# A diffusion backbone layer on one core: raw weights in a ring of six blocks, a later place for the post norm's transposes, reordered chains at both ends

## The chip, the core and the metric

The kernel runs on one core of a Trainium2 chip. A core has five engines with a queue of instructions each: TensorE (PE, matrix products; its weight loads are shown apart as PEld), VectorE (DVE), ScalarE (ACT), GpSimd (POOL) and SyncE (SP, which here only issues DMAs). An engine takes its instructions strictly in order and waits on semaphores for the others. The time is the device time of one execution in microseconds; the number that counts is the median of several runs.

## The reference

One layer for 512 latent tokens (8 rows of 64) and 256 context tokens, width 1024, all in float32:

```python
sh, sc, gt = _modulation(c, w_mod[i], b_mod[i])
h = _rmsnorm(x, pre_g[i]) * (1.0 + sc[:, None, :]) + sh[:, None, :]
parts = _split_in(h @ w_in[i])                 # 10 parts of 1024 columns
q, k, v = rope(parts[4]), rope(parts[5]), parts[6]     # 16 heads of 64
attn = _neighbourhood_attention(q, k, v, k_c, v_c, rpb[i])
y_a = (silu(z_a) * b_gate * _dwconv3(c_gate * x_in, conv_w, conv_b)) @ w_out_conv
y_b = (silu(z_b) * attn) @ w_out_attn
merged = sigmoid(g_a) * y_a + sigmoid(g_b) * y_b
x = x + gt[:, None, :] * _rmsnorm(merged @ w_o, post_g[i])
```

The attention of a token reaches over a window of 8 x 16 tokens and all context keys in one softmax. The context tokens go through the same modulation and give keys and values only.

## The kernel before

**Precision.** Each float32 operand of a product is split into a high part H (rounded to the matmul's fp32r type by an ACT copy) and a low part L (DVE, source minus H); a product is three matmuls, H·H, H·L and L·H. `split` (lines 65 to 76) does it; a line 68 or 71 in the profile is therefore a split of anything.

**Weights.** The input and output projections come in chunks of two units of 128 columns, for all 1024 rows: 1 MB each. `Chunk` (line 84) loads a chunk as two halves `raw` of 512 KB (rows 0 to 511 and 512 to 1023; line 90), in a pool of three such buffers. A half holds, for each of its four row blocks, 256 columns; its first and last 128 columns are the blocks b11, b12 (first half) and b21, b22 (second half). There are two kinds of chunk:

- *unpaired*: `split` (line 92) makes H and L of each half at once, 128 x 1024.
- *paired* (`first`, `second`, `pair`): the two units are computed together by a scheme of seven block products instead of eight. `first` splits b11, adds b12, splits the sum, splits b21, adds b22 and splits that sum; `second` splits what is left: T3 (from b12), T4 (from b21) and B22 (from b22), and B12 ahead of them where `keep` is set. The sums are made in place in the raw blocks.

A half's buffer can be written again when the last instruction that reads or changes either of its blocks is done. `Chunks` (line 129) goes through the list `order`: it loads the next chunk in the middle of the present one (`more`) and calls its `first` one attention block later (`behind`). The split weights `w` lie in four buffers.

**Stages.** (1) In `with tc.manual_schedule` (line 456), PE, DVE, ACT and SP keep the order of the program: x is loaded and normalised, transposed on PE, scaled and shifted with the modulation (`m`, line 542), split into `hx`, and multiplied in the same loop with the first six units of weights (`steps`, line 444; weights `fraw`, split into `fH` and `fL`). The modulation itself is a dot product of w_mod's rows with silu(c) on DVE (`condition`, line 397). `crow` is c, `sp` a table of small per-channel constants; both are loaded on SP's queue (lines 457 and 459). (2) Four convolution channels, the context's modulation. (3) 64 attention blocks (8 pairs of heads, 2 heads, 4 column blocks), with the projections of the next pair filled in between by `plan`. (4) The merge: for each of 8 column blocks j (line 938) the two output projections are gated and added; beside it the weights of w_o are loaded (`load_block`), and gate and post norm's gain are combined into one vector `gains` (line 974). At j == 6 that vector is spread over all partitions: eight copies on DVE (line 989), eight PE transposes (990), two ACT copies into `gpost` (991). (5) The output projection by the same scheme of seven products (`tokens`, `both`, lines 1004 to 1017), with squares, sums and the residual (`squares`, `partial`, `close`).

Outside stage 1 a planner orders each engine's queue: it goes through a model of the run with a cost for each instruction, and gives an engine the first instruction in program order that is ready at that point of the model. On the chip the order then stands, whatever is late.

Of the kernel before, what the change touches and what calls it, by code (L numbers as in the profile page):

```python
# [15 lines left out]
P = 128  # L16
# [11 lines left out]
def layer(ctx: ExitStack, tc, xp, ctxt, ctxT, cc, wmod, small, wfirst, win, wout, wo, rel, tab, out):  # L28
# [9 lines left out]
    class Banks:  # L38


        def __init__(self, *tags):
            self.tags, self.n = tags, 0
# [38 lines left out]
    def wtile(shape):  # L81
        return wp.tile(shape, F32R, name="w", bufs=4)

    class Chunk:


        def __init__(self, src):
            self.raws = [wp.tile([P, 4, 256], F32, name="raw", bufs=3) for _ in range(2)]
            for i, raw in enumerate(self.raws):
                nc.sync.dma_start(raw, src[:, 4 * i:4 * i + 4])  # L90

        def split(self):
            t = [wtile([P, 4, 2, 256]) for _ in range(2)]
            for x, raw in zip(t, self.raws):
                split(x[:, :, 0], x[:, :, 1], raw)
            k = range(KT)
            return tuple([t[i // 4][:, i % 4, y] for i in k] for y in range(2)) + ([t[i // 4][:, i % 4] for i in k],)

        def first(self, keep=False):
            (b11, b12), (b21, b22) = self.b = [(r[:, :, :P], r[:, :, P:]) for r in self.raws]  # L100
            t, sums = (wtile([P, 2, 2, 4, P]) for _ in range(2))
            split(t[:, 0, 0], t[:, 0, 1], b11)
            nc.vector.tensor_add(b11, b11, b12)
            split(sums[:, 0, 0], sums[:, 0, 1], b11)
            split(t[:, 1, 0], t[:, 1, 1], b21)
            nc.vector.tensor_add(b11, b11, b22)
            split(sums[:, 1, 0], sums[:, 1, 1], b11)
            self.keep = keep
            if not keep:
                nc.vector.tensor_add(b12, b12, b22)  # L110
            nc.vector.tensor_add(b21, b21, b11)
            self.B = {"B11": t[:, 0], "B21": t[:, 1], "T1": sums[:, 0], "T2": sums[:, 1]}
            return self
# [15 lines left out]
    class Chunks:  # L129
# [4 lines left out]

        def load(self, n):
            if n < len(self.srcs) and n not in self.ahead and n not in self.raw:
                self.raw[n] = Chunk(self.srcs[n][0])
                if behind is None:
                    self.ready(n)
                else:  # L140
                    behind.append(lambda: self.ready(n))
# [235 lines left out]
    with ExitStack() as p0:  # L377
# [66 lines left out]
        def steps(k):  # L444
            H, L = first.pop(k)
            for i in range(6):
                cs = slice(i * P, (i + 1) * P)
                nc.tensor.matmul(acc[i], lhsT=H[:, cs], rhs=hx[0][k], start=k == 0, stop=False)  # L448
                nc.tensor.matmul(acc[i], lhsT=L[:, cs], rhs=hx[0][k], start=False, stop=False)  # L449
            for i in range(6):  # L450
                cs = slice(i * P, (i + 1) * P)
                nc.tensor.matmul(acc[i], lhsT=H[:, cs], rhs=hx[1][k], start=False, stop=k == KT - 1)  # L452
# [1 line left out]

        E = mybir.EngineType
        with tc.manual_schedule(engines={E.PE, E.DVE, E.Activation, E.SP}):
            nc.sync.dma_start(crow, cc[0:1].rearrange("o (a n) -> o a n", a=2))
            xn = [load_x(xp, i, f"x{i}", f"u{i}", hp) for i in range(4)]
            nc.sync.dma_start(sp, small)
            for k in range(3):  # L460
                load_slab(k)
                load_first(k)
# [68 lines left out]
            for k in range(KT):  # L531
                cast_first(k)
                condition(k, 0, [1])
                col = cols.pop((k, 0))
                nc.vector.tensor_mul(col[:, 0:1], col[:, 0:1], sp[:, PG + k:PG + k + 1])
                rest_first(k)
                if k == KT - 1:
                    nc.vector.tensor_scalar(out=hcv, in0=sp[:, CW:CW + 32], scalar1=0.5, scalar2=None, op0=ALU.mult)
                if k + 1 < KT:
                    condition(k + 1, 0, [0])  # L540
                m = st.tile([P, S], F32, name="m", bufs=2)
                nc.scalar.activation(m, turned_x.pop(k), AF.Identity, bias=col[:, 1:2], scale=col[:, 0:1])
                split(hx[0][k], hx[1][k], m)
                if k + 3 < KT:
                    load_slab(k + 3)
                    load_first(k + 3)
                elif k == 5:
                    after = Chunk(order[3][0])
                steps(k)
                if k + 2 < KT:  # L550
                    turned_x[k + 2] = turn_x(k + 2)
# [378 lines left out]
    def sums1(q):  # L930

        nc.vector.tensor_sub(raws[q][:, :, h1], raws[2 + q][:, :, h1], raws[q][:, :, h1])
        nc.vector.scalar_tensor_tensor(
            out=raws[q][:, :, h0], in0=raws[q][:, :, h1], scalar=-1.0, in1=raws[q][:, :, h0],
            op0=ALU.mult, op1=ALU.subtract,
        )

    for j in range(KT):
# [28 lines left out]
        if j in (4, 5):  # L967
# [3 lines left out]
            for k in range(4 * j - 16, 4 * j - 12):  # L971
# [3 lines left out]
                    out=t, in0=t, in1=cond, scale=1.0, scalar=sp[:, BM + 16 + k:BM + 17 + k],  # L975
                    op0=ALU.mult, op1=ALU.add, accum_out=gains[:, k:k + 1],
                )
        if j == 6:

            nc.vector.tensor_mul(gains, gains, sp[:, QG:QG + KT])  # L980
            nc.vector.tensor_scalar(out=gains[:, 0:4], in0=gains[:, 0:4], scalar1=0.5, scalar2=None, op0=ALU.mult)
            nc.vector.tensor_scalar(out=gains[:, 4:8], in0=gains[:, 4:8], scalar1=-0.5, scalar2=None, op0=ALU.mult)
            gpost = bp.tile([P, D], F32, name="gpost")
            for i in range(2):
                gb = cv.tile([P, S], F32, name="ta")
                ps = pj()
                for k in range(4):
                    n = 4 * i + k
                    nc.vector.tensor_copy(gb[:, k * P:(k + 1) * P], gains[:, n:n + 1].broadcast_to([P, P]))
                    nc.tensor.transpose(ps[:, k * P:(k + 1) * P], gb[:, k * P:(k + 1) * P], ident)  # L990
                nc.scalar.copy(gpost[:, i * S:(i + 1) * S], ps)
        if j == 5:
            sums1(0)
        if j == 6:
            nc.scalar.activation(const.tile([P, 1], F32, name="dummy2"), G[7][:, 1, :1], AF.Sqrt, bias=eps, scale=0.0)
            wB11 = moving(B11)
# [29 lines left out]
    def snap(dst, ps):  # L1026
        return lambda t: nc.scalar.copy(dst[:, t], ps[t])

    def squares(t, cols, n, src):
        nc.scalar.activation(sq[:, :cols.stop - cols.start], src, AF.Square, accum_out=sums[:, t, n:n + 1])  # L1030
        nc.vector.tensor_mul(ys[t][:, cols], src, gpost[:, cols])

    def added(a, b):
        y = cv.tile([P, S], F32, name="ta")[:, :a.shape[-1]]
        nc.vector.tensor_add(y, a, b)
        return y
# [71 lines left out]
    for i in range(2):  # L1108
        cols = slice(256 * i, 256 * (i + 1))
        if i == 0:  # L1110
            ff = pj()[:, :256]
            tokens(None, a22, wT4, True, 1, cols, ff)
            squares(3, cols, 1, added(U3s[:, 1, cols], ff))
            partial(3, 1, False)
        else:
            tokens(fa[1], a22, wT4, False, 1, cols)
            squares(3, cols, 2, fa[1][:, cols])
# [87 lines left out]
```

## Time and profile before

| what | value |
|---|---|
| median of 3 runs | 710.05 us (708.62 to 710.88) |
| profiled execution | 710.26 us, its span 708.4 us |
| granted TensorE clock | 0.997 |
| PE busy | 693.9 us, 98% |
| DVE busy | 602.1 us, 85% |
| ACT busy | 446.2 us, 63% |
| POOL busy | 66.9 us, 9% |
| loads of raw weights | 90 of 512 KB (74 from w_in, 16 from the output projections) |

A row of the timeline is: start in us, duration in us, engine, line, operation, output and inputs, number of instructions merged, and in brackets the idle time of the engine before it with what ended it. SPq is SP's queue, which is where a DMA is issued. In the view of waits, a row has the waiting instruction, what it waited for, the total in us, how often, and the longest. In groups by line, the figures after the bar are busy time in us, the mean of one in ns, the idle time before them, and what ended it. A row of windows has the length, then busy time and number of instructions for PE, PEld, DVE, ACT and POOL, the granted clock, the DMA engines' busy share and GB/s. The rows for DMA issues end with KB each and the median us from issue to landing.

### The profile page before, as it was taken

The numbers are of one execution on the slowest core, as the hardware profiler recorded it, in microseconds if no ns is written. First come the engines' busy times: TensorE is split into PE (matmuls) and PEld (weight loads), VectorE is DVE, ScalarE is ACT, GpSimd is POOL, SyncE is SP. The second block draws the span as 40 slices with busy tenths as digits, with TensorE's granted clock in tenths as the row PEclk, the third lists the DMA queues.
The fourth block names the chain that finished last, engine by engine and source line by source line (L and its number), as shares of the span: only waits on it lengthen the run. The fifth ranks groups of instructions, "written<-read, shape, count | busy, mean of one in ns | idle before, by whom it ended". The sixth has DMA issues, their size and how long they took to land.

```text
span 708.4 us, 11705 instructions
## 1 busy us (share of the span) xinstructions
PE 693.9 (98%) x4304; PEld 621.7 (88%) x4304; DVE 602.1 (85%) x1154; ACT 446.2 (63%) x895; POOL 66.9 (9%) x110
## 2 busy tenths in 40 slices
PE   7999999999999999999999999999999999999996
PEld 4888888889979999898999989998898899987885
DVE  6999998679897898978898797998898676669997
ACT  6577543567777687774885766877694444434563
POOL 0000003131030210302203113000000000000000
PEclk9999999999999999999999999999999999999998
DMA  8995855445352473452626436313733233695013
GB/s 341 406 342 201 293 183 127 118 106 138 111 129 66 110 219 108 103 152 62 166 94 176 107 115 148 100 60 106 251 113 123 84 115 120 204 347 192 31 59 119
DMA packets 37613, 108.81 MB, mean 154 GB/s; under 512 B 5042, under 2 KB 5298, under 8 KB 37556
## 3 DMA queue, kind: packets, MB, share of 16 engines
q1 hardware_dynamic: 29092, 92.73, 38.3%
q0 software_dynamic: 8320, 15.21, 10.8%
q8 instruction: 34, 0.56, 0.3%
q14 instruction: 23, 0.19, 0.1%
q10 hardware_dynamic: 144, 0.13, 0.1%
HBM read 87.60 MB, written 5.25 MB: 131 GB/s over the span
## 4 chain that ended last, share of the span: by engine, by line
PE 79%; DVE 10%; DMA 7%; ACT 2%; issue 1%; SPq 1%; POOL 0%; DVEq 0%; ACTq 0%
PE ps L290 24%; PE ps L167 8%; PE ps L166 8%; PE ps L165 8%; PE ps L178 6%; PE ps L1009 5%; PE ps L765 3%; PE ps L183 3%; PE ps L746 3%; DVE w L71 3%; DMA raw<-in_win 3%; PE ps L709 2%; PE ps L448 2%; PE ps L452 2%; PE ps L449 2%; PE ps L197 2%
## 5 line engine op out<-in xcount | busy, mean ns | idle before, releaser
L68 ACT CAST w<-raw 128x512 fp32r<-128x512 f32 (+1 forms) x209 | 143.5, 711 | 98.4 <-PE ps L167 36.5
L71 DVE TENSOR_TENSOR w<-raw,w 128x512 fp32r<-128x512 f32 (+1 forms) x209 | 163.6, 797 | 40.6 <-ACT w L68 39.7
L290 PE MATMUL ps<-S,w 128*128 128x256 f32 x1104 | 140.3, 283 | 0.4 <-ACT tc L301 0.4
L290 PEld LDWEIGHTS ps<-S,w 128*128 128x128 f32 x1104 | 135.8, 192 | 0.8 <-ACT tc L301 0.6
L290 PE MATMUL ps<-h,w 128*128 128x256 f32 x828 | 107.9, 284 | 0.0
L290 PEld LDWEIGHTS ps<-h,w 128*128 128x128 f32 x828 | 103.4, 191 | 1.8
L165 PE MATMUL ps<-h,w 128*128 128x512 f32 x160 | 62.6, 391 | 0.0
L167 PE MATMUL ps<-h,w 128*128 128x512 f32 x160 | 62.5, 391 | 0.0
L166 PE MATMUL ps<-h,w 128*128 128x512 f32 x160 | 62.3, 389 | 0.0
L618 POOL DMA_DIRECT2D tc<-tb x32 | 28.8, 1213 | 284.7 <-DVE tc L616 252.7
L739 ACT ACTIVATE pt<-pt,z 128x512 f32<-128x512 f32 x64 | 43.0, 722 | 8.0 <-DVE z L737 7.7
L71 DVE TENSOR_TENSOR TL<-ps,TH 128x512 fp32r<-128x512 f32 x64 | 42.0, 679 | 1.6 <-ACT TH L68 1.3
L725 DVE CUSTOM_DVE_ANT_1 ps<-ps,bt 128x512 f32<-128x512 f32 x56 | 38.5, 691 | 3.5 <-PE ps L709 3.4
L68 ACT CAST TH<-ps 128x512 fp32r<-128x512 f32 x64 | 35.6, 586 | 8.3 <-PE ps L746 8.1
L167 PEld LDWEIGHTS ps<-h,w 128*128 128x128 f32 x160 | 30.0, 188 | 6.3
L165 PEld LDWEIGHTS ps<-h,w 128*128 128x128 f32 x160 | 30.1, 188 | 6.2
L166 PEld LDWEIGHTS ps<-h,w 128*128 128x128 f32 x160 | 30.0, 188 | 6.2
L746 PE MATMUL ps<-ident,pt 128*128 128x128 f32 x256 | 33.4, 273 | 1.2 <-ACT pt L739 1.2
L178 PE MATMUL ps<-w,h 128*128 128x512 f32 x128 | 32.4, 394 | 0.0
L746 PEld LDWEIGHTS ps<-ident,pt 128*128 128x128 f32 x256 | 29.2, 140 | 3.5 <-ACT pt L739 1.8
L732 ACT ACTIVATE pt<-ps,m 128x512 f32<-128x512 f32 x32 | 22.1, 689 | 12.8 <-DVE m L725 12.1
L765 PE MATMUL ps<-TL,V 128*128 128x256 f32 (+1 forms) x96 | 27.9, 320 | 1.3 <-DVE TL L71 1.3
(249 smaller groups left out, 1404.4 us busy)
## 6 DMA issues: line engine op xcount, KB each, us to landing
raw<-in_win SPq DMA_DIRECT2D x74, 512.0 KB, 4.3
wm<-in_wmod SPq DMA_DIRECT2D x26, 512.0 KB, 8.3
raw<-in_wout SPq DMA_DIRECT2D x16, 512.0 KB, 4.8
bt<-in_rel SPq DMA_DIRECT2D x16, 256.0 KB, 2.7
tc<-tb POOLq DMA_DIRECT2D x32, 128.0 KB, 3.0
B<-in_wo SPq DMA_DIRECT2D x8, 512.0 KB, 7.4
wg<-in_wmod SPq DMA_DIRECT2D x8, 512.0 KB, 5.3
fraw<-in_wfirst SPq DMA_DIRECT2D x8, 384.0 KB, 8.5
```

The lines of the kernel that those rows point to most:

```text
L68: cast = nc.scalar.copy(H, src)
L71: nc.vector.tensor_sub(L, src, H.bitcast(F32))
L165: nc.tensor.matmul(ps, lhsT=H[k][:, cs], rhs=mH[k], start=k == 0, stop=False)
L166: nc.tensor.matmul(ps, lhsT=H[k][:, cs], rhs=mL[k], start=False, stop=False)
L167: nc.tensor.matmul(ps, lhsT=L[k][:, cs], rhs=mH[k], start=False, stop=k == KT - 1)
L178: nc.tensor.matmul(ps, lhsT=mH[k][:, ts], rhs=both[k].rearrange("p a c -> p (a c)"), start=k == 0, stop=False, skip_group_check=True,)
L290: nc.tensor.matmul(ps, lhsT=w[:, x, k], rhs=act[y][k], start=start and k + o == 0, stop=k == 3 and o == 2, skip_group_check=True,)
L725: nc.vector.tensor_tensor_reduce(out=s3, in0=s3, in1=bt[:, e::4 - e][:, 0:2], scale=-1.0, scalar=3.0e38, op0=ALU.add, op1=ALU.min, accum_o ...
L739: nc.scalar.mul(x, x, z[:, i:i + 1])
L746: nc.tensor.transpose(tp[:, c], pt[:, c * P:(c + 1) * P], ident)
L765: nc.tensor.matmul(o3[:, dst], lhsT=V[p][:, kt, h], rhs=src(t), start=n == 0 and t is TH, stop=n == len(work) - 1 and t is TL,)
L1009: nc.tensor.matmul(out, lhsT=a(x, k, ts), rhs=w[y][k // 2][:, k % 2, cols], start=start and k + o == 0, stop=k == 3 and o == 2, skip_group ...
```

## The change

- **Ring.** The three raw buffers of 512 KB become one tile `ring` of six blocks of 256 KB. A chunk takes the next four blocks in turn. The arrays in HBM are rearranged on the host so that each block (512 rows by 128 columns) lies contiguous. A paired chunk is loaded by four DMAs, one a block; an unpaired chunk by two DMAs of two blocks as before.
- **Front.** `crow` is loaded from ACT's queue and `sp` from POOL's. In `steps` the six matmuls with the high weights come first, then six with the low ones. ACT writes `hx[0]` straight from the transposed x, then `m` by a second activation; DVE subtracts.
- **Merge.** The block that spreads `gains` (three small DVE operations, eight copies, eight transposes, two ACT copies) is at j == 7 instead of j == 6. `sums1(0)` stays at j == 5.
- **End.** For the first half of the last tokens' last columns, the partial sum of squares stands between the square on ACT and the multiplication on DVE, not behind both.

```diff
+    ring = wp.tile([P, 6, S], F32, name="ring", bufs=1)
+    turn = [0]
     class Chunk:
-        def __init__(self, src):
-            self.raws = [wp.tile([P, 4, 256], F32, name="raw", bufs=3) for _ in range(2)]
-            for i, raw in enumerate(self.raws):
-                nc.sync.dma_start(raw, src[:, 4 * i:4 * i + 4])
+        def __init__(self, src, blocks=False):
+            self.raws = []
+            for i in range(2):
+                at = 2 * (turn[0] % 3)
+                turn[0] += 1
+                for o, n in ((0, 1), (1, 1)) if blocks else ((0, 2),):
+                    nc.sync.dma_start(ring[:, at + o:at + o + n], src[:, 2 * i + o:2 * i + o + n])
+                self.raws.append(ring[:, at:at + 2].rearrange("p u (k c) -> p u k c", k=4))
         def split(self):
...
-                split(x[:, :, 0], x[:, :, 1], raw)
+                H, L = (x[:, :, y].rearrange("p k (u c) -> p k u c", u=2) for y in range(2))
+                split(H, L, raw.rearrange("p u k c -> p k u c"))
...
-            (b11, b12), (b21, b22) = self.b = [(r[:, :, :P], r[:, :, P:]) for r in self.raws]
+            (b11, b12), (b21, b22) = self.b = [(r[:, 0], r[:, 1]) for r in self.raws]
...
-                self.raw[n] = Chunk(self.srcs[n][0])
+                self.raw[n] = Chunk(*self.srcs[n])
...
                 nc.tensor.matmul(acc[i], lhsT=H[:, cs], rhs=hx[0][k], start=k == 0, stop=False)
+            for i in range(6):
+                cs = slice(i * P, (i + 1) * P)
                 nc.tensor.matmul(acc[i], lhsT=L[:, cs], rhs=hx[0][k], start=False, stop=False)
...
-            nc.sync.dma_start(crow, cc[0:1].rearrange("o (a n) -> o a n", a=2))
+            nc.scalar.dma_start(crow, cc[0:1].rearrange("o (a n) -> o a n", a=2))
...
-            nc.sync.dma_start(sp, small)
+            nc.gpsimd.dma_start(sp, small)
...
-                nc.scalar.activation(m, turned_x.pop(k), AF.Identity, bias=col[:, 1:2], scale=col[:, 0:1])
-                split(hx[0][k], hx[1][k], m)
+                tp = turned_x.pop(k)
+                for x in (hx[0][k], m):
+                    nc.scalar.activation(x, tp, AF.Identity, bias=col[:, 1:2], scale=col[:, 0:1])
+                nc.vector.tensor_sub(hx[1][k], m, hx[0][k].bitcast(F32))
...
-        if j == 6:
+        if j == 5:
+            sums1(0)
+        if j == 7:
             nc.vector.tensor_mul(gains, gains, sp[:, QG:QG + KT])
...
-        if j == 5:
-            sums1(0)
...
-    def squares(t, cols, n, src):
+    def squares(t, cols, n, src, then=lambda: None):
         nc.scalar.activation(sq[:, :cols.stop - cols.start], src, AF.Square, accum_out=sums[:, t, n:n + 1])
+        then()
         nc.vector.tensor_mul(ys[t][:, cols], src, gpost[:, cols])
...
-            squares(3, cols, 1, added(U3s[:, 1, cols], ff))
-            partial(3, 1, False)
+            squares(3, cols, 1, added(U3s[:, 1, cols], ff), lambda: partial(3, 1, False))
...
+    def by_block(w):
+        w = w.reshape(-1, 128, 2, 4, 2, 128).transpose(0, 1, 2, 4, 3, 5)
+        return np.ascontiguousarray(w).reshape(-1, 128, 4, 512)
+    win, wout = by_block(win), by_block(wout)
```

## The prediction

> **What bounds the kernel now.** I read the busy times first, then what the TensorE (PE) waited for.
>
> ```profile
> PE 693.9 (98%) x4304; PEld 621.7 (88%) x4304; DVE 602.1 (85%) x1154; ACT 446.2 (63%) x895; POOL 66.9 (9%) x110
> ```
>
> PE idles 14.5 us of the 708.4 us span. The view of waits says for whom:
>
> ```profile
> ...
> PE ps L765 <- DVE TL L71: 1.3, 1, 1.3
> PE ps L746 <- ACT pt L739: 1.2, 1, 1.2
> PE ps L448 <- ACT h L68: 1.1, 1, 1.1
> PE ps L709 <- ACT pt L736: 0.5, 1, 0.5
> PE ps L990 <- DVE ta L989: 0.4, 1, 0.4
> PE ps L290 <- ACT tc L301: 0.4, 1, 0.4
> ```
>
> The rows make 4.9 us, 1.1 before the first product and 3.8 in the middle; the rest of the idle time is the start-up and the end. A matmul's end is modelled, so a gap costs more than its idle time:
>
> ```profile
> L165 PE MATMUL ps<-h,w 128*128 128x512 f32 x160 | 62.6, 391 | 0.0
> 663.74 11.04 PE L1009 MATMUL ps<-w,A 128*128 128x512 f32 x48
> ```
>
> 48 matmuls in 11.04 us is 0.23 us each, while one is drawn 0.39 long: 0.16 us is added to each gap in the middle. The kernel is thus PE-bound, and no part of the change removes a matmul: it can gain only at the gaps, at the front and behind the last matmul.
>
> **The front.** The timeline of the first 20 us, not all rows:
>
> ```profile
> 0.74 1.28 ACT L468 ACT_TABLE_LOAD   x1 [0.74 <-PEq L1194]
> 0.74 0.34 SPq L457 DMA_DIRECT2D crow<-in_cc  x1
> 1.14 1.78 SPq L383 DMA_DIRECT2D x<-in_xp  x4
> ...
> 13.46 0.83 ACT L432 CAST fH<-fraw 128x768 fp32r<-128x768 f32 x1 [0.72 <-DMA fraw<-in_wfirst]
> 13.99 0.15 DVE L535 TENSOR_TENSOR col<-col,sp 128x1 f32<-128x1 f32 x1
> ...
> 15.06 0.62 ACT L68 CAST h<-m 128x512 fp32r<-128x512 f32 x1
> 15.73 0.51 PE L448 MATMUL ps<-h,fH 128*128 128x512 f32 x1 [1.12 <-ACT h L68]
> 18.47 0.78 ACT L542 ACTIVATE m<-ps,col 128x512 f32<-128x512 f32 x1 [0.61 <-DVE col L535]
> ```
>
> The chain into the first product is load, cast fH, m (0.78, as in the row of 18.47), cast h. With crow off SP, x is issued at 0.74 instead of 1.14, and all loads behind it come 0.40 earlier (taking sp's issue off SP too only shortens a queue whose data wait in line anyway). So fH runs 13.06 to 13.85, col is ready at 13.75, and ACT writes h straight from the transposes: 13.85 + 0.78, PE at about 14.7. Gain 1.0; I take **0.95**. If the loads do not come earlier, only the cast's 0.62 goes. If ACT loads its table ahead of the issue of crow, all behind Silu is up to 1.28 late: a loss of 0.33. I take the issue to come first, since the table load carries the line of the activation.
>
> The second activation (0.78 for m) replaces the cast (0.62): 8 times 0.16 us of ACT, beside PE. Taking the six L products behind the six H products gives fL 6 times 0.23 us more time; no matmul is added. The next h follows ACT's 18.47: 0.40 earlier plus 0.78, near 18.9, against PE's need at 15.73 - 1.0 + 4.6 (22 matmuls) = 19.3, so the gain holds by 0.4 us. sp now goes through POOL, which has nothing to do there; it is wanted at about 10 us.
>
> **The ring.** The split of a paired chunk has four raw blocks: b11, b12 in one half, b21, b22 in the other. Before, a half (512 KB) is loaded when both its blocks are free; after, each 256 KB block of a paired chunk waits for its own place. b21 of a chunk then goes where b11 of the chunk before was, which the first step of that chunk's split already freed; b22 still waits for the T3 split of b12. For unpaired chunks nothing is freed sooner, but loads queued behind them are shorter. Loads, then the three places at which late raw data ends in a PE gap:
>
> ```profile
> raw<-in_win SPq DMA_DIRECT2D x74, 512.0 KB, 4.3
> bt<-in_rel SPq DMA_DIRECT2D x16, 256.0 KB, 2.7
> ```
> ```profile
> 188.43 5.87 SPq L90 DMA_DIRECT2D raw<-in_win  x4
> 191.64 1.05 ACT L68 CAST w<-raw 128x1024 fp32r<-128x1024 f32 x1 [1.67 <-DMA raw<-in_win]
> 195.24 0.62 ACT L68 CAST w<-raw 128x512 fp32r<-128x512 f32 x1 [1.60 <-DMA raw<-in_win]
> 201.15 1.27 PE L746 MATMUL ps<-ident,pt 128*128 128x128 f32 x8 [1.17 <-ACT pt L739]
> ...
> 227.98 1.54 SPq L90 DMA_DIRECT2D raw<-in_win  x2
> 232.40 0.69 DVE L110 TENSOR_TENSOR raw<-raw 128x512 f32<-128x512 f32 x1 [1.62 <-DMA raw<-in_win]
> ...
> 479.39 1.53 SPq L90 DMA_DIRECT2D raw<-in_win  x2
> 484.32 0.62 ACT L68 CAST w<-raw 128x512 fp32r<-128x512 f32 x1 [1.50 <-DMA raw<-in_win]
> ```
>
> At 191 an unpaired half is late (1.67): that stays. The b11 behind it is late by 1.60 at 195: as 256 KB, issued before 189, it lands near 192.5 and the wait goes. PE's two gaps there (0.5 + 0.16, 1.17 + 0.16) are 2.0 us; ACT and DVE are 1.6 sooner, I keep 0.1 for the queue: **1.5**. At 232 DVE's in-order queue stands for b22: 256 KB issued at 227.98 lands 2.7 later, 230.7, and DVE's 1.62 go; the PE gap at L290 behind it (0.4 + 0.16) closes: **0.6**. At 484 ACT waits for b21, whose place was free long before 479.39: the 1.50 go, of which DVE, in order behind ACT's cast, gets most, and the gap at L765 (1.3 + 0.16) shrinks: **1.2**. Each lies between nothing (the next item in the same queue is late instead) and the whole gap. Sum 3.3, bounds 0 and 4.0.
>
> The price: the 23 paired chunks load in 92 DMAs instead of 46, 0.33 us of SP each by the issues above, 15 us in 570 on a queue that mostly waits. That the blocks now lie contiguous saves nothing to speak of:
>
> ```profile
> L71 DVE TENSOR_TENSOR w<-raw,w 128x512 fp32r<-128x512 f32 x165 | 110.1, 684 | 22.1 <-ACT w L68 21.5
> L71 DVE TENSOR_TENSOR TL<-ps,TH 128x512 fp32r<-128x512 f32 x64 | 42.0, 679 | 1.6 <-ACT TH L68 1.3
> ```
>
> The first reads rows of 128 out of 256, the second contiguous data: 5 ns in 684, on an engine beside PE.
>
> **The merge.** The transposes of the post norm's vector:
>
> ```profile
> 652.91 0.33 PE L990 MATMUL ps<-ident,ta 128*128 128x128 f32 x1 [0.45 <-DVE ta L989]
> 653.93 0.85 PE ps L990 x7
> 657.73 4.62 DVE L918 TENSOR_TENSOR T<-B,B 128x1024 f32<-128x1024 f32 x4
> 664.54 0.68 DVE L945 SCALAR_TENSOR_TENSOR g<-g,ps 128x512 f32<-128x512 f32 x1
> 668.68 0.68 DVE L952 TENSOR_TENSOR g<-g 128x512 f32<-128x512 f32 x1
> ```
>
> The gap there costs 0.45 + 0.16 = 0.6. One block later the copies L989 stand behind the totals L918 and behind L945 and L952 of block 7 in DVE's program order. DVE's work up to that point is the same, so they end where L952 ends now, 669.4. PE, without the gap and the 8 transposes (0.9), ends block 7 at 663.74 - 1.5 = 662.2. If the planner puts the transposes behind the 24 or more products that follow (5.5 us), little or nothing waits; but ACT's copies to gpost fall where ACT and DVE feed these products just in time, so the 0.6 is not kept safely. If they stand right behind block 7, PE waits 7.0. Bounds: gain 0.6, loss 6.4; I take **0**, nearest to the present row.
>
> **The end.**
>
> ```profile
> 702.81 0.15 DVE L1043 SCALAR_TENSOR_TENSOR sums<-sums 128x1 f32<-128x1 f32 x1
> 702.88 0.42 DVE L1031 TENSOR_TENSOR ys<-ps,gpost 128x256 f32<-128x256 f32 x1
> 703.06 0.29 ACT L1047 ACTIVATE sums<-sums 128x1 f32<-128x1 f32 x1 [0.28 <-DVE sums L1043]
> 703.38 0.17 DVE L1048 RECIPROCAL sums<-sums 128x1 f32<-128x1 f32 x1
> ```
>
> With the partial sum ahead of the multiplication ACT starts its root 0.28 sooner, but the reciprocal still stands behind both multiplications, until 702.88 + 0.34 = 703.22: gain **0.15** (0 to 0.28).
>
> **Sum.** 0.95 + 3.3 + 0 + 0.15 = 4.4 us off the profiled 710.26 (span 708.4 and 1.9 around it): 705.85. The median of 710.05 lies 0.2 below the profiled run: **705.7**.
>
> **Rivals.** *Every gap closes*: front 1.1, ring 4.0, merge 0.6, end 0.3: 6.0, so 704.0. For it: each gap has a cause that the change moves. Against: PE would need all sources in time at once.
>
> *The ring brings nothing*: b11 or b22 still arrives late because four DMAs follow each other, or another split stands in the same place. 710.05 - 1.1 (front and end) = 709.0. For it: 4.3 us for 512 KB and 2.7 for 256 KB make two blocks in turn dearer than one half, 5.4. Against: in the rows at 188 and 479 the issues follow before the first lands, so loads overlap. The Trainium skill ("DMA: Bandwidth & Descriptors", Rules for kernel authors) asks for 1 MiB or more per DMA for full bandwidth; by that rule the halved loads would side with this rival. The two rows here cannot decide it.
>
> *The transposes stop PE behind block 7*, as priced above: +6.4 - 4.4 = +2.0, 712.0, slower. It decides where PE's order puts them ahead of the products by over 4.4 us of DVE's lag. For it: DVE reaches L945 at 664.54 although PE has passed it. Against: the planner sees the same long DVE work.
>
> *The ring is tracked as one tile*, so that each load waits for all readers. This speaks for it: bt is one tile with two halves, and its loads wait for readers:
>
> ```profile
> SPq L701 <- DVE m L725: 82.4, 13, 27.8
> 440.00:460.00 20.00, 20.00 (x162) 19.52 (x161) 19.95 (x42) 17.00 (x36) 2.05 (x4) 1.00 0.38 105
> ```
>
> Against: bt's readers reach over both halves with one stride, the blocks do not. Each paired chunk then starts 2.7 us later; where DVE has no free time (19.95 of 20), three chunks make 8 us, with the ring's 3.3 lost: 717.
>
> **Chances.** Forecast 0.52, all gaps 0.15, ring nothing 0.17, transposes 0.11, one tile 0.05. What a measurement tells from no change is 0.3%, 2.1 us: faster is below 707.9, slower above 712.2. The first two are faster but for 0.02 of the forecast's upper end; ring nothing is the same; the transposes are split: faster 0.65, same 0.24, slower 0.11. The likeliest case alone spans 703.8 to 708.3; the range, down to all gaps closed less 1.1 us of spread and up to the transposes at full price, is 702.9 to 712.0.
>
> **What would show it.** The first L448 near 14.7; no wait of ACT or DVE on raw above 0.5 us at the three places, and DMA waits of ACT on raw below half of now; no PE gap at L709, L746, L765; L990 among the L1009 products without a gap. Wrong if PE's gaps in the middle again sum to over 4 us, above all one at L990 or at a raw-fed product.

## The result and the profile after

The changed kernel takes **707.7 us** (median of 18 runs, 706.26 to 709.71); the kernel before, run beside it, takes 711.31 us (18 runs, 708.62 to 715.96). The ratio is **0.9946, 95% interval 0.9931 to 0.9961**: 0.54% faster, 3.8 us (2.8 to 4.9). The forecast was 4.4 us off the time before. The profiled execution takes 708.75 us, its span 706.8 (before 710.26 and 708.4). The one lies 1.05 above the median of its kernel, the other 1.05 below, so that the two spans differ by 1.5 us only and show less than the medians do.

The diff moves the lines: the projections' products L290 are now L299, the attention's L709, L746 and L765 are L722, L759 and L778, the steps L448 are L457, the merge's copies and transposes L989 and L990 are L1004 and L1005, the output products L1009 are L1022, the squares L1030 are L1043. Busy times and PE's waits after (waiting instruction, what it waited for, total us, how often, longest):

```profile
PE 692.9 (98%) x4304; PEld 621.3 (88%) x4304; DVE 602.6 (85%) x1154; ACT 444.4 (63%) x895; POOL 67.5 (10%) x111
...
PE ps L507 <- ACT crow L479: 3.7, 1, 3.7
PE ps L1022 <- DVE w L71: 1.3, 2, 1.1
PE ps L759 <- ACT pt L752: 0.7, 1, 0.7
PE ps L722 <- DMA ks<-kl: 0.6, 1, 0.6
PE ps L457 <- ACT h L555: 0.6, 1, 0.6
PE ps L206 <- ACT tc L321: 0.4, 1, 0.4
PE ps L299 <- ACT tc L310: 0.2, 1, 0.2
```

The waits at the scores behind `pt` (L709 before), at L765 and at the transposes L990 are gone. The one at L746 fell from 1.2 to 0.7. Three are new: at the output products L1022, at L722 behind a DMA of POOL's queue that copies `kl` into `ks`, and at L206. The waits of ACT and DVE for raw weights show the ring at work. Before:

```profile
ACT w L68 <- DMA raw<-in_win: 22.0, 20, 2.1
...
ACT w L68 <- DMA raw<-in_wout: 11.4, 5, 6.0
...
DVE raw L110 <- DMA raw<-in_win: 3.2, 3, 1.6
```

After (DVE's row is gone), and the loads of w_in by size, with the median from issue to landing:

```profile
ACT w L68 <- DMA ring<-in_wout: 21.8, 5, 9.8
...
ACT w L68 <- DMA ring<-in_win: 3.2, 4, 1.2
...
ring<-in_win SPq DMA_DIRECT2D x92, 256.0 KB, 3.0
ring<-in_win SPq DMA_DIRECT2D x28, 512.0 KB, 4.2
```

In the attention, where w_in is loaded, 25.2 us of ACT's and DVE's waiting became 3.2. ACT's waits for w_out grew from 11.4 to 21.8 us; they lie in the merge, and PE has no gap there until the output products. The table of starts in the trace says where the span went (the last attention transpose closes stage 3):

| us from the span's start | first product L448/L457 | last attention transpose | last product | span |
|---|---|---|---|---|
| before | 15.73 | 501.52 | 701.92 | 708.4 |
| after | 14.57 | 498.59 | 700.10 | 706.8 |

1.16 us were gained up to the first product and 1.77 in the attention; merge and output gave 1.1 back, and the end another 0.3. One profile of each kernel is a thin base for that, as the experiments show. Both traces hold 4304 matmuls, so the n-th of one can be set against the n-th of the other. The lead of the changed kernel, by these starts:

| behind | time before, us | lead, us |
|---|---|---|
| the first product | 15.7 | 1.16 |
| a short new wait at L299 (157.72 after) | 162 | 0.66 |
| the gaps near 200 | 204 | 1.17 |
| the new wait at L722 (222.94 after) | 228 | 0.49 |
| the gap at 246 | 267 | 1.40 |
| the gap at 487 | 494 | 2.93 |

The three places of the ring gave 0.51, 0.91 and 1.53, together 2.95 us; two new waits took 1.19 back. The front after:

```profile
0.74 0.53 ACTq L468 DMA_DIRECT2D crow<-in_cc  x1
0.74 1.82 SPq L392 DMA_DIRECT2D x<-in_xp  x4
1.30 1.28 ACT L479 ACT_TABLE_LOAD   x1 [1.30 <-PEq L1213]
...
12.14 0.82 ACT L441 CAST fH<-fraw 128x768 fp32r<-128x768 f32 x1
13.48 0.16 DVE L546 TENSOR_TENSOR col<-col,sp 128x1 f32<-128x1 f32 x1
13.74 0.78 ACT L555 ACTIVATE h<-ps,col 128x512 fp32r<-128x512 f32 x1 [0.79 <-DVE col L546]
14.57 1.66 PE L457 MATMUL ps<-h,fH 128*128 128x512 f32 x6 [0.55 <-ACT h L555]
```

The issue of crow goes ahead of the table load and x is issued 0.40 earlier. ACT, done with fH at 12.96, waits for `col`, which is the last to come. But the issue has its price on ACT: the table load starts at 1.30 instead of 0.74, the activation of crow at 2.60 instead of 2.25, and PE waits 3.7 us for its result (above). Before, it was:

```profile
PE ps L496 <- ACT crow L468: 3.4, 1, 3.4
```

The three places of the ring, after:

```profile
187.58 8.95 SPq L97 DMA_DIRECT2D ring<-in_win  x6
193.39 1.05 ACT L68 CAST w<-ring 128x1024 fp32r<-128x1024 f32 x1 [1.17 <-DMA ring<-in_win]
194.60 1.14 ACT L68 CAST w<-ring 128x512 fp32r<-128x512 f32 x2
194.76 2.11 PE L206 MATMUL ps<-hc,w 128*128 128x512 f32 x8 [0.41 <-ACT tc L321]
200.60 0.66 PE L759 MATMUL ps<-ident,pt 128*128 128x128 f32 x4 [0.71 <-ACT pt L752]
...
230.76 0.69 DVE L119 TENSOR_TENSOR ring<-ring 128x512 f32<-128x512 f32 x1
...
483.78 2.17 ACT L68 CAST w<-ring 128x512 fp32r<-128x512 f32 x4
```

At 230.76 DVE adds b22, and at 483.78 ACT casts b21, with no wait for a load, and PE has no gap behind either. At 193.39 the half of the unpaired chunk is still late, and cast 1.75 us later than before (191.64) although PE came to this place 0.7 earlier. Windows of the trace suggest why (length, PE, PEld, DVE, ACT, POOL busy, granted clock, share of the DMA engines, GB/s). Before, then after:

```profile
188.00:190.00 2.00, 2.00 (x17) 1.91 (x16) 1.90 (x4) 1.95 (x3) 0.00 (x0) 1.00 0.31 90
```
```profile
188.00:190.00 2.00, 2.00 (x17) 1.91 (x17) 1.86 (x3) 1.09 (x2) 0.00 (x0) 1.00 0.68 222
```

The half is issued at 188.43 before and at 188.47 after; it lands after 3.2 us before and after 4.9 us after. Blocks whose place came free earlier, issued from 186.36 on, are now under way at the same time; ACT splits the first of them at 194.60. The likely reading is that data that nobody waited for yet went ahead of the data that ACT needed next.

Merge and output after:

```profile
659.42 2.36 DVE L931 TENSOR_TENSOR B<-T,B 128x1024 f32<-128x1024 f32 x2
664.77 1.22 DVE L71 TENSOR_TENSOR w<-B,w 128x1024 fp32r<-128x1024 f32 x1
666.05 1.66 PE L1022 MATMUL ps<-w,A 128*128 128x512 f32 x6 [1.10 <-DVE w L71]
667.79 1.17 DVE L1004 COPY ta<-gains 128x128 f32<-128x128 f32 x8
667.93 0.50 PE L1022 MATMUL ps<-w,A 128*128 128x512 f32 x1 [0.22 <-DVE w L71]
668.26 1.08 PE L1005 MATMUL ps<-ident,ta 128*128 128x128 f32 x8
```

The transposes stand among the output products without a gap. PE, which reached these products at 659.11 instead of 663.74, now waits there for a split of DVE. The end before, then after:

```profile
702.30 0.38 ACT L1030 ACTIVATE cs<-ps 128x256 f32<-128x256 f32 x1 [0.52 <-PE ps L1009]
703.58 1.54 DVE L1050 SCALAR_TENSOR_TENSOR ys<-ys,sums,xr 128x512 f32<-128x512 f32 x3
```
```profile
700.77 0.38 ACT L1043 ACTIVATE cs<-ps 128x256 f32<-128x256 f32 x1 [0.82 <-PE ps L1022]
...
701.81 1.54 DVE L1064 SCALAR_TENSOR_TENSOR ys<-ys,sums,xr 128x512 f32<-128x512 f32 x3
```

From the last square to the closing instructions it is 1.04 us instead of 1.28. But that square begins 0.67 behind the last product's start, 0.38 before, and the span does not get the gain. How much of this is the edit's is told with the end alone.

### The profile page after: what moved, and what is told of

It reads as the page before. It is cut to its first block, busy times and chain, and to the rows that moved or that the text cites. A ratio compares the mean times of both kernels' runs of the same rounds, so it can differ in the third digit from the quotient of the medians.

```text
span 706.8 us, 11837 instructions
## 1 busy us (share of the span) xinstructions
PE 692.9 (98%) x4304; PEld 621.3 (88%) x4304; DVE 602.6 (85%) x1154; ACT 444.4 (63%) x895; POOL 67.5 (10%) x111
## 4 chain that ended last, share of the span: by engine, by line
PE 79%; DVE 8%; DMA 7%; issue 3%; ACT 1%; SPq 1%; POOL 0%; DVEq 0%; ACTq 0%; POOLq 0%
PE ps L299 28%; PE ps L174 7%; PE ps L175 7%; PE ps L176 7%; PE ps L187 5%; PE ps L1022 4%; PE ps L778 3%; PE ps L759 3%; PE ps L192 3%; PE ps L722 3%; DVE w L71 2%; PE ps L457 2%; PE ps L463 2%; PE ps L460 2%; PE ps L206 2%
## 5 line engine op out<-in xcount | busy, mean ns | idle before, releaser
L71 DVE TENSOR_TENSOR w<-ring,w 128x512 fp32r<-128x512 f32 (+1 forms) x209 | 163.7, 798 | 37.9 <-ACT w L68 37.1
L68 ACT CAST w<-ring 128x512 fp32r<-128x512 f32 (+1 forms) x209 | 142.1, 712 | 80.8 <-DMA ring<-in_wout 21.8
L299 PE MATMUL ps<-S,w 128*128 128x256 f32 x1104 | 140.3, 283 | 0.2 <-ACT tc L310 0.2
L299 PEld LDWEIGHTS ps<-S,w 128*128 128x128 f32 x1104 | 135.8, 192 | 0.4 <-ACT tc L310 0.4
L299 PE MATMUL ps<-h,w 128*128 128x256 f32 x828 | 108.1, 284 | 0.0
L299 PEld LDWEIGHTS ps<-h,w 128*128 128x128 f32 x828 | 103.6, 191 | 1.9
L759 PE MATMUL ps<-ident,pt 128*128 128x128 f32 x256 | 33.3, 272 | 0.7 <-ACT pt L752 0.7
L759 PEld LDWEIGHTS ps<-ident,pt 128*128 128x128 f32 x256 | 29.2, 140 | 2.9 <-ACT pt L752 1.1
L778 PE MATMUL ps<-TH,V 128*128 128x256 f32 (+1 forms) x96 | 28.4, 318 | 0.0
```

Of the source, the lines that this page charges most:

```text
L68: cast = nc.scalar.copy(H, src)
L71: nc.vector.tensor_sub(L, src, H.bitcast(F32))
L299: nc.tensor.matmul(ps, lhsT=w[:, x, k], rhs=act[y][k], start=start and k + o == 0, stop=k == 3 and o == 2, skip_group_check=True,)
L759: nc.tensor.transpose(tp[:, c], pt[:, c * P:(c + 1) * P], ident)
L778: nc.tensor.matmul(o3[:, dst], lhsT=V[p][:, kt, h], rhs=src(t), start=n == 0 and t is TH, stop=n == len(work) - 1 and t is TL,)
```

## The experiments

Each kernel is the one before or the changed one with the edit shown. Each ratio is to the kernel before on the same chip, with its 95% interval. The starts of the profiles, those with totals on POOL apart, stand in one table at the end.

**Front alone.** Both parts of it, with the raw buffers, the merge and the end as before.

```diff
-            nc.sync.dma_start(crow, ...)
+            nc.scalar.dma_start(crow, ...)
-            nc.sync.dma_start(sp, small)
+            nc.gpsimd.dma_start(sp, small)
...
-                nc.scalar.activation(m, turned_x.pop(k), ...)
-                split(hx[0][k], hx[1][k], m)
+                for x in (hx[0][k], m):
+                    nc.scalar.activation(x, tp, ...)
+                nc.vector.tensor_sub(hx[1][k], m, ...)
```

> The front part alone (crow from ACT's queue, sp from POOL's, h written straight by ACT, low weights after the high ones). Theory: the kernel is bound by PE, so what the first product gains (1.16 us earlier in the changed kernel's profile) is carried through all stages in which PE has no gap: first product at about 14.6, span 0.7 to 1.2 us shorter than 708.4, ratio about 0.9985. Rival: the later stages stand on DVE and loads and not on PE; then the last product of the attention stage is earlier by less than 0.5 us and the ratio is 1.000.

Ratio 1.0003 (0.9979 to 1.0028), median 711.44: no change that can be seen. The prediction's term, 0.95 us or 0.13%, lies within the interval, which reaches from a gain of 1.5 us to a loss of 2.0. This profiled execution (712.42 us) holds something that the one before does not. Its PE waits at the raw-fed place, and the windows behind:

```profile
PE ps L713 <- ACT pt L740: 1.6, 1, 1.6
PE ps L750 <- ACT pt L743: 1.2, 1, 1.2
...
200.00:205.00 5.00, 3.23 (x13) 2.70 (x14) 4.99 (x12) 3.02 (x8) 3.21 (x4) 0.73 0.52 105
205.00:210.00 5.00, 5.00 (x28) 4.28 (x28) 4.09 (x10) 4.78 (x14) 2.11 (x5) 0.93 0.52 96
```

After the two gaps, 2.8 us together, the granted clock falls. Taken as a fall to one half, the two windows hold (0.27 + 0.07) x 5 / 0.5 = 3.4 us of it, and the trace's record of the granted clock has one half from 202.32 to 205.73; in that stretch matmuls start 0.43 us apart instead of 0.23. So 3.4 us are worked at half pace, 1.7 us lost beyond the gaps.

**Ring alone.** The class `Chunk` and the arrays as in the change, all else as before.

> The ring alone. Theory: the stretch from the first product of the projections to the last transpose of the attention blocks takes 447.8 us instead of 449.5, as in the changed kernel, and PE's gaps in it sum to about 2.5 us instead of 4.6; part of it is lost again in the merge, where PE then arrives earlier at DVE's work: span 0.7 to 1.8 us shorter. Rival, the ring brings nothing: the gaps in the attention stage sum to over 4 us again and the ratio is 1.000.

Ratio **0.9957 (0.9942 to 0.9972)**, median 708.12: 3.1 us (2.0 to 4.1) of the change's 3.8. The ring is most of the change; the intervals leave open how much the rest adds. The profiled span is 705.8, 2.6 less than before and more than the 0.7 to 1.8 that were expected; in the attention PE's waits fall from 3.4 us to 1.2.

**Merge alone, end alone.** The post norm's transposes one block later; the partial sum ahead of the multiplication.

```diff
-        if j == 6:
+        if j == 7:
             nc.vector.tensor_mul(gains, gains, sp[:, QG:QG + KT])
```
```diff
         nc.scalar.activation(sq[...], src, AF.Square, ...)
+        then()
         nc.vector.tensor_mul(ys[t][:, cols], src, gpost[:, cols])
```

> The merge part alone (transposes of the post norm's vector one column block later). Theory: the gap of 0.6 us at the transposes goes, but DVE's work up to the second group of output products is the same, so that PE waits 0.2 to 0.6 us there; span within 0.4 us of 708.4, ratio 1.000. Rival, the transposes now stop PE or their copies delay the splits: a gap of over 1 us at the output products, span over 709.2.

> The end part alone (partial sum ahead of the multiplication). Theory: from the start of the last square on ACT to the first of the last three residual additions on DVE it takes 1.04 us instead of 1.28, and nothing else moves: 0.2 us, not to be told in the time (ratio 1.000). Rival: the last square starts later after PE's last product, as in the changed kernel (0.67 us after its start instead of 0.38), because of this edit; then the span does not shorten.

Merge: ratio 1.0006 (0.9983 to 1.0029). The gap at the transposes is gone, and two small ones at the output products (L1009 <- DVE w, 0.4 us in two) have come, as in the changed kernel. End: 0.9988 (0.9969 to 1.0006). Neither can be told from no change. With the end alone the last square starts 0.38 behind the last product, as before, and 1.10 us pass to the closing additions instead of 1.28: the edit gains 0.18 there. The changed kernel's 0.67 and 1.04 are not the edit's, for the ring alone, which lacks it, has 0.67 and 1.03. The profile of the end alone has a gap of 1.8 us at the transposes L990, where the kernel before has 0.4 from the same code: that gap differs by over a microsecond from one execution to the next.

**Ring, front and end, without the moved transposes.**

> The whole change without its merge part: the transposes of the post norm's vector stay at block 6. In the changed kernel PE's gaps in the merge and output stage grew from 0.6 to 1.65 us, at output products that wait for DVE's splits. Theory: this is DVE's own pace (PE arrives 3 us earlier at the same work), so the gaps stay, at the transposes or at the output products, 1.2 to 2 us in sum, and the time is that of the changed kernel, within 0.6 us. Rival: the moved copies (1.2 us on DVE between the splits) make the gaps; then they fall to 0.6 and this kernel is 1 us faster than the changed one, ratio about 0.993.

Ratio 0.9951 (0.9935 to 0.9967), median 707.52: as the full change. The output stage of this profile has no gap at all:

```profile
660.98 11.07 PE L1021 MATMUL ps<-w,A 128*128 128x512 f32 x48
```

So in this pair of profiles the moved copies bring the gaps at L1022. The times do not follow: what the move costs at L1022 it may save at the old place, where the last two kernels below have a wait of 1.6 us each. The front's gain went here:

```profile
PE ps L205 <- ACT tc L320: 1.2, 1, 1.2
...
194.28 1.04 ACT L68 CAST w<-ring 128x1024 fp32r<-128x1024 f32 x1 [2.16 <-DMA ring<-in_win]
```

This load was issued at 188.37 and landed 5.9 us later. In this profile the unpaired half sets the pace there.

**Ring, but loads of halves.** The ring's tile and the contiguous blocks stay; every chunk loads by two DMAs of 512 KB.

```diff
-                self.raw[n] = Chunk(*self.srcs[n])
+                self.raw[n] = Chunk(self.srcs[n][0])
```

> The ring alone, but each half of every chunk is loaded by one DMA of 512 KB, which waits for both its places, as before the change; layout and ring stay. Theory: what shortens the attention stage is that a block is loaded when its own place is free; without it PE's gaps there are those of before, 4 us or more in sum, and the ratio is 1.000. Rival: the ring, the contiguous blocks or another order of the queues does it; then the stage takes 447.8 us as with the ring alone.

Ratio 1.0007 (0.999 to 1.0025): the whole gain is gone. ACT's waits are nearly back to what they were before, and with them a gap of PE and the half clock:

```profile
ACT w L68 <- DMA ring<-in_win: 20.2, 17, 2.9
PE ps L717 <- ACT pt L744: 2.1, 1, 2.1
...
200.00:205.00 5.00, 3.33 (x11) 2.72 (x12) 4.53 (x13) 2.67 (x6) 3.36 (x4) 0.70 0.99 233
205.00:210.00 5.00, 5.00 (x32) 4.54 (x32) 3.77 (x7) 4.76 (x12) 0.21 (x1) 0.96 0.13 23
```

Neither the single tile nor the layout in HBM gains anything; loading and releasing block by block does. The traces show both sides of it. At the second place the first load goes out at 226.97 after the change and at 227.98 before, at the third at 476.99 and 479.39; PE's lead alone makes 0.5 and 1.4 of that. These loads land after 2.5 and 2.7 us instead of 4.3 and 4.9. So a block starts earlier and also arrives faster, and by these rows the second is the larger part. No run separates the two.

**Two totals on POOL**, in the changed kernel and in the one without the moved transposes: DVE is relieved of four of the eight additions of w_o's blocks.

```diff
-            total(T3, B12, B22)
+            total(T3, B12, B22, nc.gpsimd)
...
-            total(T4, T2, B21)
+            total(T4, T2, B21, nc.gpsimd)
```

> The whole change, and four of the eight sums of w_o's blocks (T3 and T4, 128x1024 each, 1.13 us apiece on DVE) go to the idle POOL. Theory: DVE's pace sets the merge's last part, so 4.5 us less work on it closes PE's gaps at the output products (1.65 us): 1.0 to 1.7 us faster than the changed kernel, ratio about 0.992. Rival: the gaps come from elsewhere, or POOL's sums come too late for the later splits or slow DVE's own work: no gain or a new gap.

> As the run with the four sums on POOL, but with the transposes left at block 6. If DVE's pace alone decides, the two agree within 0.6 us; if the place of the transposes matters by itself, this one keeps a gap of 0.5 us or more at the transposes and is that much slower.

Ratios 1.0100 (1.0081 to 1.0119) and 1.0043 (1.0026 to 1.0059): slower by 7.1 and 3.1 us than the kernel before, where a gain had been expected. Of the first:

```profile
PE ps L1004 <- DVE ta L1003: 7.4, 1, 7.4
...
658.66 2.80 DVE L930 TENSOR_TENSOR T<-B,B 128x1024 f32<-128x1024 f32 x1
661.38 4.03 DVE L71 TENSOR_TENSOR A<-g,A 128x512 fp32r<-128x512 f32 x3
...
657.23 3.14 POOL L930 TENSOR_TENSOR B<-T,B 128x1024 f32<-128x1024 f32 x1 [7.14 <-DVE T L930]
661.59 2.67 POOL L930 TENSOR_TENSOR B<-T,B 128x1024 f32<-128x1024 f32 x1 [1.22 <-issue]
...
663.00:668.00 5.00, 1.12 (x4) 1.03 (x5) 5.00 (x10) 1.23 (x2) 1.26 (x1) 0.53 0.00 0
668.00:673.00 5.00, 5.00 (x22) 3.90 (x22) 4.51 (x11) 3.84 (x7) 0.00 (x0) 0.79 0.32 105
```

The transposes stand one product behind block 7, and PE waits 7.4 us: the third rival as it was priced, in a kernel where the planner's order goes that way. DVE begins the copies for them at 666.61, no later than in the changed kernel (667.79), so the wait comes from PE's order in the first place. POOL did not relieve DVE either. An addition on DVE beside one on POOL takes 2.80 us instead of 1.2, and three splits 4.03 instead of the 1.89 that they take in the changed kernel. DVE's addition ends 1.1 us behind POOL's (661.46 and 660.37), about one addition's time. The Trainium skill ("SBUF — State Buffer", SBUF: two separate sides) says that VectorE, reading two inputs, and GpSimd share a pair of ports that the one which starts first locks for its whole instruction; these rows agree. The half clock covers (0.47 + 0.21) x 5 / 0.5 = 6.8 us here, and 6.8 in the second kernel behind a gap of 4.1.

**The change again, and two variants beside it**, on one chip: the changed kernel itself; ring, shorter steps and end with crow and sp still on SP's queue; ring, front and end with every chunk loaded by blocks.

```diff
-                self.raw[n] = Chunk(*self.srcs[n])
+                self.raw[n] = Chunk(self.srcs[n][0], True)
...
-                    after = Chunk(order[3][0])
+                    after = Chunk(order[3][0], True)
```

> The changed kernel once more, as the measure for the two beside it. Both theories (the late moved copies of the merge cost something; they cost nothing) expect 0.993 to 0.996 of the kernel before. If the moved copies cost what the gaps of 1.26 and 0.39 us in the changed kernel's output stage suggest, the kernel with ring, front and end alone stays 0.5 us or more below this one over many executions; so far the two were 0.9951 and 0.9946, which says no difference. What this run adds is whether the wait of the products for VectorE's splits is there again.

> Ring, the earlier and shorter steps of the front, and the end; crow and sp stay on SP's queue, the merge as before. Theory 1, the front's gain is swallowed at the load of the unpaired chunk near 190 us and not by the two queues: the first product comes at 14.6 to 15.2 us, the attention's last transpose near 498.6 to 499, and the time is 707.3 to 708.2, ratio 0.995 to 0.996, as with the two queues moved. Theory 2, moving crow and sp is what gives the front its gain: the first product comes at 15.3 or later, and the time is no better than the ring alone, 708.1. Theory 3, the two queues cost time by holding the x loads up: better than both, 706.5 or less.

> Ring, front and end, and every chunk loaded block by block (256 KB), the unpaired ones too, which elsewhere load in halves of 512 KB. Theory 1, the gap that is left near 194 us (1.36 us with ring, front and end) is the unpaired chunk's half, whose load took 5.89 us and began when both of its blocks were free: a block can start as soon as one is free, so the gap falls below 0.5 us, the attention's last transpose comes 0.8 us earlier or more, and the time is 706.3 to 707.0, ratio 0.993 to 0.994. Theory 2, VectorE's split ahead of the load sets that place: both blocks come free together, and the two transfers side by side take as long as one of twice the size; gap 1.0 us or more and time 707.3 to 707.8. A loss (708 or above) would say that the smaller transfers cost queue time that the halves do not.

Ratios 0.9954 (0.9937 to 0.9972), 0.9957 (0.9941 to 0.9973) and 0.9969 (0.995 to 0.9988). The change holds; its wait at L1022, 1.3 us in the first profile, is 0.2 in this one. Moving crow and sp off SP shows no gain: with the old queues the first product comes at 14.91, within the 14.57 to 15.26 of the kernels with the new ones. Loading everything by blocks does what was expected at its place in the trace (the unpaired half is cast at 192.03 instead of 193.39, the gap near 194 is gone, one of 1.2 us before 199.24 stays, and the attention ends earliest of all), and its profiled span is the shortest; but its median is 708.57, not the 706.3 to 707.0 that were expected for that case, and not below the others. Its 12 executions fall into four of 706.04 to 707.21 and eight of 708.29 to 709.76, and the profiled one, 707.12, is of the first group: what the eight lose, no trace here shows. No run here beats the changed kernel clear of the intervals.

| us from the span's start | first product | last attention transpose | last product | span |
|---|---|---|---|---|
| front alone | 15.26 | 503.84 | 704.08 | 710.6 |
| ring alone | 15.45 | 498.92 | 699.19 | 705.8 |
| merge alone | 15.13 | 501.84 | 702.94 | 709.4 |
| end alone | 15.11 | 501.12 | 702.84 | 709.1 |
| ring, front, end | 14.59 | 499.19 | 699.13 | 705.6 |
| ring, loads of halves | 15.32 | 504.86 | 705.09 | 711.5 |
| the change again | 15.00 | 499.12 | 699.23 | 705.9 |
| ring, shorter steps, end | 14.91 | 498.37 | 700.26 | 706.6 |
| all by blocks | 14.57 | 497.66 | 699.17 | 705.3 |

## Why the prediction was right, and where not

**The bound.** Right: no matmul fell away, PE stays at 98%, and the gain came at gaps. The time itself lies 2.0 us above the forecast of 705.7; 1.3 of that is the kernel before, whose median over 18 runs is 711.31 and not the 710.05 of three.

**The front, 0.95: mis-sized.** The first product came at 14.57, as forecast (near 14.7), and the issue of crow went ahead of the table load, as taken. But the term was a difference to one row, 15.73, and that row was a late one: the five profiles without the edit average 15.35 (15.73, 15.45, 15.13, 15.11, 15.32), the seven with all of it 14.89 (14.57, 15.00, 15.26, 14.59, 14.57, and 15.15 and 15.11 with totals on POOL). That is 0.46 us. The step that failed is "all loads behind it come 0.40 earlier". From the end of `col` to the first product the seven take 0.94 us and the five 1.58, so the cast's 0.62 went as worked out. But `col` itself is ready at 13.96 in the seven and at 13.77 in the five: not earlier. What the prediction put at nothing is what the move costs crow itself: ACT's activation of it starts at 2.6 to 3.2 us in the seven, either behind the later table load or waiting for crow to land (front alone, 3.20), and at 2.2 to 2.5 in the five. PE's wait for it grows from 3.4 to 3.6 us to 3.7 to 4.3, and ACT's work that leads to `col` stands behind. And the rest does not show in the time: 1.0003 alone, and on the ring 0.9946 to 0.9957 with it against 0.9957 without. Part of it is used up near 157 and at 222 (the table of leads), part at the unpaired half near 190; the intervals cannot tell 0.5 us from nothing.

**The ring, 3.3: right in size, and that in part by luck.** Alone it gives 3.1 us (2.0 to 4.1), and the run with halves shows that the finer loads are the cause. At 232 and 484 the waits and PE's gaps went, as worked out. At 191 to 201 the step "that stays", for the unpaired half, was wrong: the half came later, most likely because blocks freed earlier shared the DMA engines with it. By the starts of matmuls, the gaps there went from 0.67 + 1.34 to 0.57 + 0.88 us, so 0.56 instead of the 1.5 counted. The gaps at 246 and 486, which closed, gave 0.8 and 1.4 where 0.6 and 1.2 were counted. That makes 2.8 us, and the two new short waits, which the prediction did not count, took 1.2 of it back in this pair of profiles. On the other side stands a term that the prediction put at nothing, the half clock avoided, some 0.7 to 1.0 us by the executions counted in the last section.

**The merge, 0: right, by another way.** The transposes found a place among the products without a gap, as foreseen; the expected trouble at gpost did not come. What took the 0.6 back in this profile was PE's earlier arrival at splits that DVE, with the same work as before, delivered no sooner. That is not always so: with the transposes at the old place two profiles have no gap in merge and output (the ring alone; ring, front, end) and two have one of 1.6 us, and the times do not tell the two places apart. The third rival did not happen, and the run with totals on POOL shows that it was a real one.

**The end, 0.15: right where it can be seen, not in the time.** The edit gains 0.18 us in the end alone, where the last square starts as before. In the changed kernel that square starts 0.29 later, as it does with the ring alone, and from the last product to the first of the closing additions it takes 1.71 us, with the ring alone 1.70. From the last product to the span's end it takes 6.4 to 6.6 us in five profiles without the edit (mean 6.49) and 6.2 to 6.7 in eight with it (mean 6.52).

**The rivals.** "The ring brings nothing" fell: a block of 256 KB lands after 3.0 us, a half of 512 KB took 4.3, and a block's place comes free sooner. The Trainium skill's row that would have sided with that rival ("DMA: Bandwidth & Descriptors", Rules for kernel authors: 1 MiB or more per DMA) speaks of the highest bandwidth; here the time until the awaited block is there decided. "One tile" fell by ACT's waits for w_in, 3.2 instead of 22.0 us. "Every gap closes" was not reached: about 3.8 us of waits in the middle became 3.2, in other places. Of the signs named in the prediction three failed: the gap at L746 (now L759) stays and L709 (now L722) has a new one, ACT still waits 1.17 us at the first of the three places, and its waits for raw weights are far below half for w_in but not for w_out.

## What to carry to other kernels

In a prefetch ring, let the transfer be as fine as the release: ask for each buffer which part is free first and which is needed first, and load that part by itself. Then look at what the earlier loads collide with, for the block that is needed next may now share the DMA engines with one that is needed later. A term that rests on one row of one profile, as the front's did, has that row's scatter; several profiles of unrelated variants show how wide it is. And an issue that is moved to another queue costs time there too: look at what stands behind it.

## What the runs showed of the hardware

A gap of PE can cost more than its length. After a wait of 2.1 us (loads of halves), or of 1.6 and 1.2 with little between them (front alone), the granted clock went to a half for 3.4 us; after 4.1 and 7.4 us (totals on POOL) for 6.8 us. Single waits of up to 1.8 us (end alone, at L990) and a pair of 1.4 and 1.2 (merge alone, at L709 and L746) did not set it off. The Trainium skill ("TensorE: Matmul & The Clock Gate", What's actually happening) describes such a clock, half or full, set in windows of 3.4 us; the lengths found here are one and two of these. The Trainium skill's advice to avoid gaps above some 3 us (same page, Why this matters for your kernels) is too lax for this trace: 2.1 us was enough once.

Where the border lies can be narrowed from the traces. In each of them the changes of the granted clock lie whole multiples of 3.41 us apart, which gives a grid of stretches. PE's idle time within one such stretch, in the middle of the kernel:

| kernel | waits | idle in the stretch, us of 3.41 | clock behind it |
|---|---|---|---|
| merge alone | 1.4, 1.2 | 1.63, then 0.94 | full |
| end alone | 1.8 | 1.82 | full |
| loads of halves | 2.1 | 2.15 | half |
| front alone | 1.6, 1.2 | 2.17 | half |

So the border in these traces is between 1.82 and 2.15 us. These rows fit if the idle time within one stretch counts: the two waits of the merge alone, 2.6 us together, are parted by the grid. The grid lies differently in each trace (a stretch begins at 196.8 us in one and at 198.9 in another), so the same waits may cost something in one execution and nothing in the next.

The executions bear this out, for each has a mean granted clock on record. The kernels that load halves (the one before, front, merge and end alone, and loads of halves) have 0.996 or less in 42 of 124 executions. Those that load paired chunks by blocks, without POOL's totals, have 0.997 to 0.999 in all 67, which the half clock behind the last product alone can give (0.997 and 0.998 in their profiles, where the clock falls nowhere else). Over all chips, the 42 take 712.7 us in the mean, the other 82 take 710.5 (the 61 of them with 0.998 or more, 710.3), the 67 take 707.9. So at like clock the blocks gain some 2.5 us, and the executions of lower clock add 0.7 to 1.0 to the mean of the halves (711.2). The kernels that load halves also scatter more (up to 717.80 with the merge alone, where the others lie between 706.0 and 709.9). In the profiles they have PE waits of 1.7 to 2.8 us in all between 197 and 203 us, the others at most 1.2. The half clock is not all of that scatter: executions of up to 713.74 us have 0.999, and what made them longer is open.
